# Output projections in two superblocks of tokens, with weight pieces split early and kept in DRAM

## The chip, the cores and the metric

The kernel runs on one core of a Trainium2 chip. The metric is the device time of one execution in microseconds (us). The core has a matrix engine (TensorE, PE in the profile), a vector engine (VectorE, DVE), a scalar engine (ScalarE, ACT), a general engine (GpSimd, POOL), and SyncE (SP), which here only issues transfers. Sixteen DMA engines move data between DRAM and the on-chip memory.

## The reference

One layer of a streaming encoder over 2048 prompt tokens and 32 sample tokens, width 1024, all in fp32. Cut to what matters (`attend` is windowed attention with 8 query and 2 key heads):

```python
(q, k, v, gate_a, b_gate, c_gate, u_in, gate_c, merge_a, merge_c) = jnp.split(h @ w_in, split_idx, axis=-1)
attn, new_k, new_v = attend(q, k, v, sink)                    # q, k normalised and rotated before
conv = ...                                                    # causal, three taps, over c_gate * u_in
y_a = (attn * jax.nn.silu(gate_a)) @ w_attn_out               # 512 -> 1024
y_c = (b_gate * conv * jax.nn.silu(gate_c)) @ w_conv_out      # 512 -> 1024
r = x + (jax.nn.sigmoid(merge_a) * y_a + jax.nn.sigmoid(merge_c) * y_c) @ w_o
r = r + jax.nn.sigmoid(r @ w_ple_gate) * (p @ w_ple_proj)
```

## The kernel before, in words

**Precision and pieces.** Each fp32 product is made of three matmuls on parts of reduced mantissa (fp32r): high weights by high rows, high by low, low by high. So every operand is split: ACT casts the high part, DVE subtracts it to get the low part (the helper at L206 and L207 in phase 1; the planner's operations all stand at one line, L135). A weight piece is 128 x 512 fp32, 256 KB, and serves 12 matmuls per block of tokens. It is loaded raw into one of 8 buffers (`wr`, pool count "wf"), then split into one of 5 tiles (`w`, `WB = 5`).

**Phase 1** (0 to about 855 us) is the big input projection, in two halves of the tokens. It uses a Strassen product (7 block products for 8). The first half runs 21 groups, each of 7 products of 12 matmuls with 512 columns; the second half nests a second level with 264 columns. The order is written by hand (`steps`). At chosen steps (`sums_at`) `quad_sums(x, n)` prepares the Strassen weights of `w_o` (x = UO = 50) and `w_ple_gate` (x = UPG = 58): it loads four quarters, adds them on DVE in four combinations, and stores the four sums to DRAM (`qs`, by POOL's DMA queue). Before, this happens at groups 1 to 8 of the first half.

**Phase 2** (about 855 us to the end) is everything behind. A planner, which runs while the program is built, writes the order of all engines. It keeps a list of events with due times (`begin`), walks the list `plan` of matmul units, and places vector work, transfers and weight loads around them by planned durations and by counts of free buffers. A transfer has a fixed planned time. The units are: yB (the convolution branch), pp (`p @ w_ple_proj`), yA (the attention branch), o (`@ w_o`) and pg (`@ w_ple_gate`). Attention runs as side work, in 17 tiles of 128 tokens (one of them the 32 sample tokens), whose matmuls S (scores), PT (transposes) and O (values) are scattered between the units. A tile's result `at` is stored to DRAM (`z_at`). When a block of tokens is complete, its four rows are loaded again (`acf`), split into `ac_h` and `ac_l` and used by yA of this block.

**Blocks before.** Tokens are cut in four blocks: 512, 512, 512 and 544 (with the sample). Block 0 makes o and pg directly (8 output rows, 8 x 3 matmuls of 512 columns each). Blocks 1 and 2 make a 2 x 2 Strassen product together (`run_big`, `big_done`, `big_end`; matmuls `b50_n_p` for o, `b58_n_p` for pg, product p, output row n; 512 columns). Block 3 makes a Strassen product of its own with 272 columns (`quad_unit`, `run_quads`, `row_quads`; matmuls `s50a` to `s50d` and `s58a` to `s58d`), with the weights loaded and split once more. Both read the sums `qs` from DRAM and split them in phase 2.

Of the kernel before, what the change touches and what calls it, by code (L numbers as in the profile page):

```python
# [13 lines left out]
P = 128  # L14
# [8 lines left out]
BLOCKS = [(0, 512, 0), (512, 512, 0), (1024, 512, 0), (1536, 512, TS)]  # L23
T3 = 1536
W = 512 + TS
# [16 lines left out]
def tile_hybrid_stream_step(ctx: ExitStack, tc: tile.TileContext, x, xT, pT, wu, consts, rope, ckT, cv_dup,  # L42
# [6 lines left out]
    tp = ctx.enter_context(tc.tile_pool(name="tp", bufs=14))  # L49
# [39 lines left out]
    limit = {"ps": 8, "P": 2, "ph": 1, "qs": 1, "q": 1, "r": 1, "z": 1, "ga": 2, "tmp": 14, "wf": 8, "k": KP, "kx": 20, "v": NV // 2 - 1}  # L89
# [98 lines left out]
    def restart():  # L188
        assert not events
        now[0], banks[0], wire[0] = 0.0, 0, None  # L190
        for x in (busy, live):
            for k in x:
                x[k] = 0
        live["k"] = 16
# [75 lines left out]
    BIG = (1, 2)  # L270
    BO = {UO: (2, 7, 1, 6, 5, 3, 4), UPG: (1, 7, 6, 5, 3, 2, 4)}
    NA = {0: range(8), 1: (4, 5, 6, 7, 0, 1, 2, 3), 2: (4, 5, 6, 7, 0, 1, 2, 3), 3: (0, 4, 1, 5, 2, 6, 3, 7)}
    plan = [("yB", e, n) for n in range(8) for e in range(2)]
    for n in range(8):
        plan += [("yB", 2, n), ("yB", 3, n), ("pp", 2, n)]
    plan += [("pp", 3, 0), ("pp", 3, 1)] + [("yA", 0, n) for n in range(5)]
    plan += [("pp", 3, 2), ("yA", 0, 5), ("pp", 3, 3), ("yA", 0, 6), ("yA", 0, 7), ("pp", 3, 4), ("pp", 3, 5)]
# [10 lines left out]
    last_parts = [[(0, 1), (0, 2), (1, 1), (1, 2)]]  # L290
    last_parts += [[x] for x in ((0, 7), (0, 6), (1, 7), (0, 5), (2, 1), (0, 3), (0, 4), (1, 6), (2, 2), (1, 5), (2, 7),
                                 (1, 3), (1, 4), (2, 6), (3, 1), (2, 5), (3, 7), (2, 3), (3, 6), (2, 4), (3, 5), (3, 2),
                                 (3, 4), (3, 3))]

    last_pg = [[(0, 1), (0, 2), (1, 1), (1, 2)]]
    last_pg += [[x] for x in ((2, 1), (2, 2), (0, 7), (0, 6), (1, 7), (0, 5), (1, 6), (0, 3), (1, 5), (0, 4), (1, 3), (2, 7), (1, 4), (2, 6), (3, 1), (2, 5),
                                (3, 7), (2, 3), (3, 6), (2, 4), (3, 2), (3, 5), (3, 4), (3, 3))]
# [24 lines left out]
    worder += [("S", UPG, n, p) for parts in last_pg for n, p in parts]
# [2087 lines left out]
```

## Time and profile before

| what | value |
|---|---|
| median of 3 runs | 1522.86 us (1521.79 to 1523.18) |
| profiled execution | 1523.18 us, of which the span from first to last instruction is 1521.4 us |
| mean granted PE clock | 0.993 of full |
| DMA | 357 MB, mean 235 GB/s |

The busy shares and the stretches are shown in the prediction. In the page, PE is the matrix engine's matmuls and PEld its weight loads, which run beside them; SPq and POOLq are the DMA issues of SyncE and GpSimd. Matmuls are pipelined: the length that the profile shows of one (0.39 us at 512 columns) is longer than the distance to the next one's start, so the distance between starts is what a matmul costs.

### The profile page before, as it was taken

Reading aid. Unit: us, or ns where it says so; the run is one execution under the profiler, and the core shown is the slowest. Engines: PE = TensorE matmul, PEld = TensorE weight load, DVE = VectorE, ACT = ScalarE, POOL = GpSimd, SP = SyncE. Lnnn points to the kernel's source line nnn. Section 1 sums busy time; section 2 is a strip of 40 time slices with the busy share of each in tenths; the row PEclk is TensorE's granted clock in tenths of the full one; section 3 lists DMA queues with packets and bytes.
Section 4 is the critical chain, followed back from the end, with each engine's and each line's share of the span. In section 5 each row is a group of like instructions: output and inputs, shape, how many; then the busy total and the mean of one; then the engine's idle time right before and its main releaser. Section 6 shows DMA issues by size and latency. Waiting matters only on the chain. (4 is left out here: it accounts for less than half of the span.)

```text
span 1521.4 us, 27059 instructions
## 1 busy us (share of the span) xinstructions
PE 1501.7 (99%) x9025; PEld 1334.0 (88%) x9025; DVE 1205.0 (79%) x2291; ACT 835.1 (55%) x1964; POOL 370.3 (24%) x533
## 2 busy tenths in 40 slices
PE   9999999999999999999999999999999999999898
PEld 7878888888889999999999989978888888889898
DVE  7897887875579776898965788789887699786786
ACT  8353254334367634443455557677776476554474
POOL 2133332332212222333223211122122312212112
PEclk9999999999999999999999999989999999999999
DMA  9479886898787946343455797777577947969999
GB/s 343 152 273 342 310 300 221 286 337 273 245 278 260 322 153 197 110 129 123 153 193 188 254 328 221 221 214 229 193 205 213 240 131 175 275 171 298 272 309 258
DMA packets 207004, 357.39 MB, mean 235 GB/s; under 512 B 24592, under 2 KB 61520, under 8 KB 206864
## 3 DMA queue, kind: packets, MB, share of 16 engines
q1 hardware_dynamic: 164928, 251.84, 51.0%
q0 software_dynamic: 32288, 85.99, 19.6%
q10 hardware_dynamic: 9648, 17.83, 3.1%
q8 instruction: 71, 1.16, 0.3%
q14 instruction: 69, 0.57, 0.1%
HBM read 238.21 MB, written 117.46 MB: 234 GB/s over the span
## 5 line engine op out<-in xcount | busy, mean ns | idle before, releaser
L599 PE MATMUL a<-x_l,w 128*128 128x264 f32 (+1 forms) x744 | 228.2, 319 | 0.0
L597 PE MATMUL a<-x_h,w 128*128 128x264 f32 (+1 forms) x744 | 227.2, 320 | 0.0
L602 PE MATMUL a<-x_h,w 128*128 128x264 f32 (+1 forms) x744 | 201.4, 320 | 0.4 <-DVE w L207 0.4
L206 ACT CAST w<-wr 128x512 fp32r<-128x512 f32 (+1 forms) x180 | 110.1, 619 | 104.7 <-PE c L602 28.8
L135 ACT CAST w<-wr 128x512 fp32r<-128x512 f32 x204 | 124.6, 620 | 75.5 <-PE yA L135 17.7
L207 DVE TENSOR_TENSOR w<-wr,w 128x512 fp32r<-128x512 f32 (+1 forms) x180 | 133.8, 753 | 35.2 <-ACT w L206 33.3
L135 DVE TENSOR_TENSOR w<-wr,w 128x512 fp32r<-128x512 f32 x204 | 139.7, 693 | 21.4 <-ACT w L135 18.5
L599 PEld LDWEIGHTS a<-x_l,w 128*128 128x128 f32 x744 | 140.0, 188 | 10.3
L597 PEld LDWEIGHTS a<-x_h,w 128*128 128x128 f32 x744 | 139.7, 188 | 10.4
L135 PE MATMUL b<-xb_h,w 128*128 128x512 f32 x448 | 142.0, 394 | 0.0
L602 PEld LDWEIGHTS a<-x_h,w 128*128 128x128 f32 x744 | 125.2, 188 | 11.2 <-DVE w L207 0.6
L735 PE MATMUL la<-x_h,w 128*128 128x264 f32 x516 | 111.8, 285 | 1.6 <-ACT w L206 1.0
L597 PE MATMUL c<-x_h,w 128*128 128x512 f32 (+1 forms) x336 | 110.5, 339 | 0.1
L599 PE MATMUL c<-x_l,w 128*128 128x512 f32 (+1 forms) x336 | 110.4, 338 | 0.0
L206 ACT CAST w<-a 128x512 fp32r<-128x512 f32 x82 | 49.7, 620 | 95.5 <-DVE a L346 33.2
L602 PE MATMUL c<-x_h,w 128*128 128x512 f32 (+1 forms) x336 | 99.9, 338 | 0.0
L135 PEld LDWEIGHTS b<-xb_h,w 128*128 128x128 f32 x448 | 83.6, 188 | 17.9
L796 DVE SCALAR_TENSOR_TENSOR u<-u,c 128x264 f32<-128x264 f32 (+1 forms) x125 | 59.4, 506 | 43.8 <-ACT u L791 27.3
L135 PE MATMUL yA<-ac_h,w 128*128 128x512 f32 (+1 forms) x320 | 90.4, 360 | 2.3 <-ACT ac_h L135 1.8
L791 ACT COPY u<-a 128x264 f32<-128x264 f32 (+1 forms) x114 | 47.4, 437 | 80.8 <-PE a L602 72.5
L735 PEld LDWEIGHTS la<-x_h,w 128*128 128x128 f32 x516 | 87.0, 189 | 2.2 <-ACT w L206 1.2
L135 PE MATMUL b<-xb_l,w 128*128 128x512 f32 x224 | 88.5, 395 | 0.0
(536 smaller groups left out, 4226.9 us busy)
## 6 DMA issues: line engine op xcount, KB each, us to landing
wr<-in_wu SPq DMA_DIRECT2D x213, 256.0 KB, 4.1
a<-in_wu SPq DMA_DIRECT2D x116, 256.0 KB, 5.1
wr<-ws SPq DMA_DIRECT2D x74, 256.0 KB, 3.4
wr<-qs SPq DMA_DIRECT2D x64, 256.0 KB, 4.8
ws<-a POOLq DMA_DIRECT2D x63, 256.0 KB, 4.0
qs<-a POOLq DMA_DIRECT2D x24, 256.0 KB, 5.8
tb<-z_t SPq DMA_DIRECT2D x24, 256.0 KB, 4.4
z_t<-tb SPq DMA_DIRECT2D x24, 256.0 KB, 4.0
```

The costliest lines, as they stand in the source:

```text
L135: return f(**kw)
L206: nc.scalar.copy(out=hi, in_=src)
L207: nc.vector.tensor_tensor(out=lo, in0=src, in1=hi.bitcast(F32), op=sub)
L597: nc.tensor.matmul(out=ps[:, :cn], lhsT=w[:, 0, k], rhs=x[0][:, c0:c0 + cn], start=first and k == 0, stop=False, skip_group_check=True)
L599: nc.tensor.matmul(out=ps[:, :cn], lhsT=w[:, 0, k], rhs=x[1][:, c0:c0 + cn], start=False, stop=False, skip_group_check=True)
L602: nc.tensor.matmul(out=ps[:, :cn], lhsT=w[:, 1, k], rhs=x[0][:, c0:c0 + cn], start=False, stop=k == 3, skip_group_check=True)
L735: nc.tensor.matmul(out=ps[:, :m], lhsT=w[:, a, k], rhs=r[:, cols], start=q in "ABG" and j == 0 and e == 0, stop=j == 1 and e == 2, skip_gr ...
L791: nc.scalar.copy(out=t[:, c0:c0 + cn], in_=ps[:, :cn])
L796: nc.vector.scalar_tensor_tensor(out=t[:, c0:c0 + cn], in0=t[:, c0:c0 + cn], scalar=-1.0, in1=ps[:, :cn], op0=mul, op1=sub)
```

## The change

1. The blocks become 512, 512, 528 and 528 tokens (`BLOCKS`), the sample inside block 2's and 3's range (`TILES`). The direct o and pg of block 0 and the code of block 3 go. o and pg are Strassen products in two superblocks `s`: blocks 0 and 1 with 512 columns, blocks 2 and 3 with 528 columns in two banks of 264. The order of the seven products changes, with 5 and 3 in pairs, and 1 and 6 too in pg; so do the sums of the results.
2. yB of all four blocks uses one set of 8 weight pieces (before one set for each two blocks). yA now has one set for each block (before blocks 1 and 2 shared one).
3. 44 weight pieces, the 32 quad sums, 8 pieces of `w_attn_out` and 4 of `w_ple_proj`, are split in phase 1 and stored to DRAM as 512 KB with both parts. `quad_sums` moves to every second group from 3 to 17; the new `keep` stands at groups 4 to 15. In phase 2 such a piece is loaded straight into a `w` tile, with no raw buffer and no split.
4. The attention tiles' start times are set anew, the rows `ac` of blocks 2 and 3 are held until a named product begins, the shared temporary pool has 15 buffers for 14, and in the second superblock some residual rows are loaded and added on DVE, where before POOL's accumulating DMA added all of them.

```diff
-BLOCKS = [(0, 512, 0), (512, 512, 0), (1024, 512, 0), (1536, 512, TS)]
+BLOCKS = [(0, 512), (512, 512), (1024, 528), (1552, 528)]
-W = 512 + TS
+W = 532
-    tp = ctx.enter_context(tc.tile_pool(name="tp", bufs=14))
+    tp = ctx.enter_context(tc.tile_pool(name="tp", bufs=15))
...
-    plan += [(kind, 0, n) for kind in ("o", "pg") for n in range(8)]
-    plan += [("yA", b, n) for n in NA[1] for b in BIG]
-    plan += [("B", UO, n, p) for p in BO[UO] for n in range(4)]
...
+    BO = {UO: (2, 1, 6, 7, 5, 3, 4), UPG: (1, 6, 7, 5, 3, 2, 4)}
+    plan = [("yB", b, n) for n in range(2) for b in range(3)] + [("yB", 3, n) for n in range(2)]
+    plan += [("yB", b, n) for n in range(2, 8) for b in range(4)]
+    first, second = products_of(0, UO), products_of(1, UO)
+    def mixed(b, parts):
+        ys = [("yA", b, n) for n in NA[b]]
+        return ys[:6] + [parts[0], ys[6], parts[1], ys[7]] + parts[2:]
+    pps = [("pp", 3, n) for n in range(8)]
+    plan += [("pp", 2, n) for n in range(8)] + pps[:4] + [("yA", 0, n) for n in NA[0]]
+    plan += first[:4] + pps[4:] + mixed(1, first[4:8]) + first[8:] + products_of(0, UPG)
+    plan += [("yA", 2, n) for n in NA[2]] + second[:4] + mixed(3, second[4:8]) + second[8:] + products_of(1, UPG)
...
         for p, o in ((7, "sc"), (5, "a21"), (6, "a11"), (3, "a12")):
-            nc.gpsimd.dma_start(out=quad_sum[x, n][:, WS[p]], in_=t[o])
+            h, lo = high(f"qh{p}_{x}_{n}"), t[o].bitcast(F32R)
+            split(h, lo, t[o])
+            nc.gpsimd.dma_start(out=quad_sum[x, n][:, WS[p], 0], in_=h.bitcast(F32))
+            nc.gpsimd.dma_start(out=quad_sum[x, n][:, WS[p], 1], in_=t[o])
+    def keep(u, e):
+        t, h = tmp(f"kr{u}_{e}")[:, :512], high(f"kh{u}_{e}")
+        nc.sync.dma_start(out=t.rearrange("p (a b) -> p a b", a=4), in_=wu[u, :, 4 * e:4 * e + 4, :])
+        split(h, t.bitcast(F32R), t)
+        nc.gpsimd.dma_start(out=kept[u, e][:, 0], in_=h.bitcast(F32))
+        nc.gpsimd.dma_start(out=kept[u, e][:, 1], in_=t)
...
-    sums_at = {(0, 1 + 2 * n + e, 6): (x, n) for n in range(4) for e, x in enumerate((UO, UPG))}
+    sums_at = {(0, 3 + 2 * (n + 4 * e), 6): (x, n) for n in range(4) for e, x in enumerate((UO, UPG))}
+    keep_at = {(0, 4 + g, 6 if g % 2 else 5): v for g, v in enumerate(kept)}
...
+                w = wp.tile([P, 2, 4, P], F32R, tag="w", name=f"w{i}")
+                W2[i] = w[:, 0], w[:, 1]
+                fin[0] = 0.0
+                eY.dma_start(out=w.bitcast(F32).rearrange("p a b c -> p a (b c)"), in_=stored_at(key))
...
+    def ac_rows(b, j):
+        while b not in ac_open:
+            yield {}
+        yield {"tmp": 1}
+        yield from split_rows(0.5, lambda: ac_pair(b, j), z_at[:, j], ("ac", b, j), b)
+    ac_open = {0, 1}
...
-            t = 11 * g if g < 4 else 33 + (e1 - 98) * (g - 3) / 8 if b < 3 else e1 - 40 + (e2 - 60 - e1) * i / (tiles - 1)
+        t = 11 * e if e < 8 else e1 - 30 + (e2 - e1) * (e - 8) / 9
+    begin.append((T[f"b0{UPG}_0_2"], lambda: ac_open.add(2)))
+    begin.append((T[f"b1{UO}_0_2"], lambda: ac_open.add(3)))
```

What the order of the instructions says at three places. The first is PE before, from the last value matmul of block 0 (O_7) to the first matmul of its yA (`yA0_0`; pp2 and pp3 are pp units of blocks 2 and 3, yB3 one of block 3; pk and pqt are transposes of another attention tile):

```order
L135 MATMUL O_7_11795<-pth_7_0_11679,VH_10072 128x256
...
L135 MATMUL S_10_0_11856<-KH_10068,qs1_1_11746 128x192
...
L135 MATMUL pp2_7_0_11866<-p0_0_h_10677,w375_11306 128x512
...
L135 MATMUL pp3_0_0_11900<-p1_0_h_11501,w377_11604 128x272
...
L135 MATMUL O_8_11959<-pth_8_0_11827,VH_10072 128x256
...
L135 MATMUL pqt1_2_12017<-cst_69,qr1_2_11837 128x128 x4
L135 MATMUL yA0_0_0_11951<-ac0_0_h_12030,w378_11624 128x512
```

After the change other units stand there, and block 1 is the first whose yA comes soon after its last value matmuls (O_15). The same engine, from O_15 to `yA1_0` (b050_3_2 is product 2 of the first superblock's o, row 3):

```order
L136 MATMUL O_15_13081<-pth_15_0_13030,VH_10320 128x256
...
L136 MATMUL b050_3_2_0_13048<-xb050_2_3_h_12851,w382_12899 128x512
...
L136 MATMUL pp3_4_0_13116<-p3_0_h_11997,w383_12938 128x264
...
L136 MATMUL pp3_7_1_13228<-p3_0_h_11997,w384_12960 128x264
...
L136 MATMUL S_18_1_13317<-KH_10316,qs2_1_13268 128x192
...
L136 MATMUL O_16_13332<-pth_16_0_13282,VH_10320 128x256
...
L136 MATMUL yA1_0_0_13241<-ac1_0_h_13293,w385_13004 128x512
```

Between them stand 3 matmuls of 512 columns, 48 pp matmuls of 264 and 37 short ones. The third place is again PE after the change, from the last value matmul of block 3 (O_31) to `yA3_0`:

```order
L136 MATMUL O_31_16305<-pth_31_0_16241,VH_10320 128x256
...
L136 MATMUL yA2_3_1_16294<-ac2_1_h_15627,w452_16069 128x264
...
L136 MATMUL b150_0_2_0_16325<-xb150_2_0_h_16094,w453_16134 128x264
...
L136 MATMUL b150_3_2_1_16442<-xb150_2_0_h_16094,w456_16285 128x264
...
L136 MATMUL yA3_0_0_16479<-ac3_0_h_16475,w457_16333 128x264
```

Between them stand the last 7 matmuls of a yA2 unit and the 96 of product 2. In phase 1, POOL's DMA queue, first before, where the four sums of one quad are stored among the stores of phase 1's own sums (`ws`):

```order
L350 DMA ws2_118<-sc2_1088 128x512
L615 DMA z_q_77<-u40_0_1076 128x512
L350 DMA ws2_118<-a2_1_1082 128x512
L364 DMA qs50_0_137<-sc_50_0_1122 128x512
L350 DMA ws2_118<-a2_0_1080 128x512
L364 DMA qs50_0_137<-a21_50_0_1116 128x512
```

The same queue after, at a later group:

```order
L360 DMA qs50_0_137<-qh7_50_0_1384 128x512
L361 DMA qs50_0_137<-sc_50_0_1379 128x512
L360 DMA qs50_0_137<-qh5_50_0_1389 128x512
L360 DMA qs50_0_137<-qh6_50_0_1394 128x512
L361 DMA qs50_0_137<-a21_50_0_1373 128x512
L628 DMA z_q_77<-u20_2_1265 128x512
```

Each sum now makes two stores, the high and the low part, and the store of the low part stands behind the DVE subtraction.

More of the change, by code (lines that the diff above doesn't have):

```diff
@@ L1365, in attention @@
         fin[0] = max(fin[0], ab_done)
-        yield {"tmp": 1} if last and i >= 3 else {}
+        yield {"tmp": 1} if out else {}
         for q, (h0, hn, src) in enumerate(q3):
@@ L1382, in attention @@
             eS.copy(out=h, in_=src)
-        if last and i >= 3:
+        if out:
             vo = tmp(f"vo{i}", cols=P)
@@ L1412, in attention @@
         yield {"ps": 2, "qs": 1}
-        if last and i >= 3:
+        if out:
             ko = kso[P - TS:P] if sample else kpo
@@ L2057, in tile_hybrid_stream_step @@
[L2057 to L2076 removed]
+            loads = [("pp", z_pp[n + 4 * i])]
@@ new lines, in big_unit @@
+            if s and (n == 3 and p in (2, 4) or p == 4):
+                loads.append(("rs", z_r[n + 4 * i]))
+        units.append(dict(b=2 * s + j, n=n, p=p, x=x, s=s, kind="B", name=f"b{s}{x}_{n}_{p}", w=[("B", s, x, n, p)],
+                          act=[()] * 4, loads=loads, got=0))
+    def run_big(u):
+        s, x, n, p = u["s"], u["x"], u["n"], u["p"]
+        g = big[s, x, n]
+        subs = blk(2 * s)[2]
+        floor[0] = 3 * len(subs)
+        fresh = p != 3 and (p != 6 or x == UO)
+        if not fresh:
+            while ("e", s, x, n, {6: 1, 3: 5}[p]) not in have:
+                idle()
+        if fresh:
+            pss = []
+            for e, (c0, cn) in enumerate(subs):
@@ L2079, in run_quads @@
                 banks[0] += 1
-                g[new] = bank(f"s{x}{new}_{n}")
-        for k in range(4):
-            for (n, p), wk in zip(u["parts"], u["w"]):
-                wi = w_of(wk, u)
-                i, half = XP[p]
-                while ("X", x, i, k) not in have or w_ready.get(wi, 1e9) > now[0]:
+                pss.append((bank(f"b{s}{x}_{n}_{p}_{e}"), c0, cn))
+            if p in (1, 5):
+                g["a"] = pss
+        else:
+            pss = g["a"]
+        wk, = u["w"]
@@ L2086, in run_quads @@
+        wi = w_of(wk, u)
+        for y, (ps, c0, cn) in enumerate(pss):
+            for k in range(4):
+                while ("XB", s, x, p, k) not in have or w_ready.get(wi, 1e9) > now[0]:
                     idle()
-                ps = groups_of[x, n]["d" if (n, p) == (3, 4) else {2: "b", 7: "c", 4: "c"}.get(p, "a")]
-                fresh = p in (1, 2, 7) or (n, p) == (3, 4)
                 hi, lo = [v[:, k] for v in W2[wi]]
-                xs = [v[:, half * m:(half + 1) * m] for v in XQ[x, k][i]]
@@ L2091, in run_quads @@
[L2091 to L2100 removed]
+                xh, xl = XB[s, x, p, k]
@@ new lines, in run_big @@
+                for e, (w, r) in enumerate(((hi, xh), (hi, xl), (lo, xh))):
+                    while begin and begin[0][0] <= work[0]:
+                        begin.pop(0)[1]()
+                    eT.matmul(out=ps[:, :cn], lhsT=w, rhs=r[:, c0:c0 + cn], start=fresh and k == 0 and e == 0,
+                              stop=k == 3 and e == 2, skip_group_check=True)
+                    work[0] += 0.00044 * cn + 0.0064
+                    due()
+                if n == 3 and y == len(pss) - 1:
+                    free("k", 2)
+                    free("kx", 2)
```

714 lines of the change are left out of this document (201 added, 513 removed).

## The prediction

> **What bounds the kernel now.** The page comes first: TensorE (PE) is busy 99% of the span. Then the windows view, because an average over the span hides where the rest is lost. PE's issue sets the time almost everywhere.
>
> ```profile
> span 1521.4 us, 27059 instructions
> PE 1501.7 (99%) x9025; PEld 1334.0 (88%) x9025; DVE 1205.0 (79%) x2291; ACT 835.1 (55%) x1964; POOL 370.3 (24%) x533
> ```
>
> ```profile
> core 0: us, PE busy (x) PEld busy (x) DVE busy (x) ACT busy (x) POOL busy (x), PEclk, DMA share, GB/s
> 60.00:100.00 40.00, 39.90 (x170) 31.46 (x169) 39.23 (x65) 23.61 (x44) 7.72 (x15) 1.00 0.50 175
> 100.00:140.00 40.00, 40.00 (x175) 32.54 (x174) 29.38 (x47) 14.43 (x26) 15.01 (x29) 1.00 0.95 342
> 220.00:260.00 40.00, 40.00 (x176) 32.31 (x175) 30.93 (x52) 19.17 (x44) 9.95 (x18) 1.00 0.64 219
> 260.00:300.00 40.00, 40.00 (x174) 32.46 (x174) 34.33 (x55) 12.39 (x22) 12.80 (x25) 1.00 0.79 277
> 300.00:340.00 40.00, 40.00 (x174) 32.39 (x174) 32.72 (x53) 17.13 (x30) 13.89 (x26) 1.00 0.95 333
> 340.00:380.00 40.00, 40.00 (x175) 32.40 (x174) 22.99 (x39) 18.02 (x32) 9.14 (x17) 1.00 0.83 281
> 996.00:1010.00 14.00, 10.91 (x39) 7.15 (x37) 8.56 (x19) 9.52 (x29) 0.00 (x0) 0.63 0.46 148
> 1368.00:1420.00 52.00, 52.00 (x317) 46.89 (x316) 36.31 (x71) 21.51 (x39) 13.24 (x16) 1.00 1.08 304
> 1420.00:1436.00 16.00, 11.40 (x68) 10.42 (x66) 15.06 (x30) 8.91 (x17) 2.62 (x3) 0.79 0.79 219
> ```
>
> Each row is a stretch: its length, busy us and instructions of each engine, granted clock, DMA share and rate. Two stretches lose time. At 996 us PE idles 14.00 - 10.91 = 3.1 us and has clock 0.63, which costs up to 14 x 0.37 = 5.2 us more. At 1420 us it idles 4.6 us and has clock 0.79, another 16 x 0.21 = 3.4 us. Together 16.3 us. The waits view of PE names them (us in total, times, longest):
>
> ```profile
> PE s50a L135 <- DVE w L135: 2.5, 1, 2.5
> PE yA L135 <- ACT ac_h L135: 1.8, 2, 1.3
> PE s50b L135 <- DVE w L135: 1.4, 1, 1.4
> PE s58b L135 <- DVE w L135: 0.5, 1, 0.5
> ```
>
> The first stretch is yA of block 0, which waits for the block's attention rows; the second is the start of block 3's o products, whose weights are not split yet.
>
> **Part 1: PE's issue.** Timeline rows of a dense 512-, 264- and 272-column stretch (start, length, instruction), then groups by form:
>
> ```profile
> 119.96 0.39 PE L597 MATMUL c<-x_h,w 128*128 128x512 f32 x1
> 120.19 0.39 PE L599 MATMUL c<-x_l,w 128*128 128x512 f32 x1
> ...
> 499.76 0.28 PE L735 MATMUL la<-x_h,w 128*128 128x264 f32 x1
> 499.88 0.29 PE L735 MATMUL la<-x_l,w 128*128 128x264 f32 x1
> ...
> 1449.91 0.29 PE L135 MATMUL s50a<-rq_h,w 128*128 128x272 f32 x1
> 1450.04 0.29 PE L135 MATMUL s50a<-rq_l,w 128*128 128x272 f32 x1
> ...
> L135 PE MATMUL b<-xb_h,w 128*128 128x512 f32 x448 | 142.0, 394 | 0.0
> L135 PE MATMUL s50a<-rq_h,w 128*128 128x272 f32 x128 | 28.3, 298 | 2.6 <-DVE w L135 2.5
> L135 PE MATMUL o<-m_h,w 128*128 128x512 f32 x128 | 42.3, 399 | 0.0
> ```
>
> Starts lie 0.23 us apart at 512 columns, 0.12 at 264, 0.13 at 272; the mean over all dense pairs of the trace is 0.2313, 0.1218 and 0.1253. The direct o and pg of block 0 are 2 x 192 = 384 matmuls of 512 columns (128 with o's high rows, 64 with the low ones, pg alike), block 3's Strassen products 672 of 272 columns. That is 88.7 + 84.0 = 172.7 us. Now blocks 2 and 3 make 1344 matmuls of 264 columns, 164.0 us, while the 672 of 512 columns (b, high and low) stay. Gain 8.7 us. Blocks 2 and 3 are now both 528 tokens in two banks, so yA and yB pay two 264s for some 512s, +0.7 us each, pp +0.3 us. **PE: -7.0 us.**
>
> A rule speaks against this term. The Trainium skill, "TensorE: Matmul & The Clock Gate", section "Back-to-back issue gap", gives about 131 ns per matmul sustained at 512 columns and 81 at 128; an estimate on the line between them is 99 ns at 264 and 272, by which the exchange would cost some 15 us (384 x 131 + 672 x 99 = 117, then 1344 x 99 = 133) instead of gaining 9. This trace does not agree: its 512s start 231 ns apart.
>
> **Part 2: the two old stalls.** In the changed order yA of block 0 comes after pp of blocks 2 and 3; PE has 20.5 us of matmuls between the block's last attention output and yA (before 10.3 us). The S start is gone; its quarter of the weights arrives split. Both stretches: **-16.3 us.** Other waits for split weights of that stage: **-1.3 us.**
>
> **Part 3: the new places of the same wait.** The chain from the last O matmul to the first yA matmul, block 0, then block 1:
>
> ```profile
> 986.22 0.28 PE L135 MATMUL O<-ptl,VH 128*128 128x256 f32 x1
> 986.99 0.56 SPq L135 DMA_DIRECT2D z_at<-at  x1
> 993.62 0.38 SPq L135 DMA_DIRECT2D acf<-z_at  x1
> 999.39 0.79 PE L135 MATMUL yA<-ac_h,w 128*128 128x512 f32 x1 [1.35 <-ACT ac_h L135]
> 1005.25 0.80 PE L135 MATMUL yA<-ac_l,w 128*128 128x512 f32 x1 [0.33 <-DVE ac_l L135]
> ...
> 1077.12 0.28 PE L135 MATMUL O<-ptl,VH 128*128 128x256 f32 x1
> 1089.97 0.65 ACT L135 ACTIVATE ac_h<-acf 128x512 fp32r<-128x512 f32 x1
> 1094.49 0.63 ACT L135 ACTIVATE ac_h<-acf 128x512 fp32r<-128x512 f32 x1
> ```
>
> It goes through DRAM (store, load, split) and takes 13.2 us to the first matmul in block 0; in block 1 13.5 us (1090.62, when ac_h is done), and 18.7 us to the last low row (1094.49 + 0.63 + about 0.7). In the changed order PE has after block 1's last O only 36 + 12 pp matmuls of 0.122, 3 of 0.231 and 37 short ones of about 0.11 before yA: 11.6 us. The fourth row is needed 3 x 0.69 us and one PT later, at 14.4 us: it is 4.3 us late. Block 3 has 7 yA and 96 b matmuls: 103 x 0.122 = 12.6 us; its fourth row is needed at 13.7 us, 5.0 us late. Block 0's 8.3 us had a gap of 10.3 us; there the fourth row (19.7 us after O) was needed at about 13.4 with the O in between, 6.3 us late, so the slowed clock added about 2 us net. With that, 6.3 and 7.0 us: **+13.3 us.** Ends: 0, if the chain runs 5 us shorter; +17, if both cost what block 0 cost.
>
> The Trainium skill, same page, section "HAM oscillation — how this bites in real kernels", has the clock fall only after PE idles more than about 3.4 us; waits of 1 to 2 us with matmuls between would leave it at full, and the two stalls would cost 9.3 us. The row at 996 us does not agree: clock 0.63 with no single wait over 1.35 us. It is kept as a rival below.
>
> **Part 4: the early splits.** Phase 1 gets 44 ACT casts and 44 DVE subtractions, 56 more POOL DMAs and 12 more SP loads, off PE's path while buffers last. The rows that price them:
>
> ```profile
> L207 DVE TENSOR_TENSOR w<-wr,w 128x512 fp32r<-128x512 f32 (+1 forms) x180 | 133.8, 753 | 35.2 <-ACT w L206 33.3
> wr<-in_wu SPq DMA_DIRECT2D x213, 256.0 KB, 4.1
> wr<-qs SPq DMA_DIRECT2D x64, 256.0 KB, 4.8
> qs<-a POOLq DMA_DIRECT2D x24, 256.0 KB, 5.8
> ```
>
> The sums move from groups 1 to 8 (about 83 to 225 us) to every second group from 3 to 17 (122 to 400 us; a group is 7 x 12 x 0.231 = 19.4 us). Per pair of groups DVE gets 4 adds, 4 + 2 subtractions, 10 x 0.6 = 6 us; so 260:300 goes from 34.3 to 40 of 40 us and its neighbours to 37 and 39. At 60:100 DVE had 39.2 of 40 and PE lost 0.1 us. The DMA gets per pair 18 x 0.262 = 4.7 MB in 38.8 us, 122 GB/s: 277 becomes 399, 333 becomes 455, 281 becomes 403. Scaled by their rows' shares these are 1.14, 1.30 and 1.19, against 1.08 at 1368:1420 with no PE loss. The excess is (3.63 - 3.24) x 40 = 16 us of DMA time. Eight raw buffers, each a piece of 12 x 0.231 = 2.8 us, less 4 us of landing, hide up to 18 us if only loads lag; the pieces summed in phase 1 and the splits have less. Ends 0 and +14; nearer 0, as buffers and the DVE row say: **+5 us.**
>
> **Part 5: pre-split loads in phase 2.** The stored pieces go by one 512 KB load straight into one of 5 tiles, without the 8 raw ones ahead. Lead: 4 x 2.77 - 0.6 = about 10.4 us. 256 KB land in 4.1 to 4.8 us by the medians above; 512 KB in about 6 by doubling the bytes' part. Late only in the crowded stretches. The ACT and DVE work they save is not on the path. SP waits for a tile's release with whatever stands behind, the attention's rows among it. Ends 0 and +10: **+2 us.** yB with one set of weights saves 8 loads and splits; hidden, 0.
>
> **Part 6: the tail.**
>
> ```profile
> 1516.08 0.29 PE L135 MATMUL s58a<-rq_h,w 128*128 128x272 f32 x1
> 1517.38 0.44 DVE L135 TENSOR_TENSOR tg<-tg,rs 128x272 f32<-128x272 f32 x1
> ```
>
> The last output row is now 528 wide after the last product instead of 272: tanh and two DVE steps at 0.65 to 0.70 (ac_h's 512 took 0.65) for 0.43 to 0.44, plus a combine: **+0.9 us.**
>
> **Sum:** -7.0 - 16.3 - 1.3 + 13.3 + 5 + 2 + 0.9 = -3.4. The profiled execution took 1523.2 us, 0.3 above the median, so 1519.8, or about **1519.5** on the median's footing.
>
> **Rivals.**
> (a) The new waits stay away. The store and reload take 5.4 us in block 1 but 6.6 in block 0; ACT and DVE are freer, and SP has fewer loads in the queue. If the rows come 5 us sooner, 13.3 us go: 1506. Against it: two blocks gave 13.2 and 13.5 us at different loads.
> (b) Slower: the DMA excess at 260 to 380 us reaches the weights. It decides from the point where pieces land more than 18 us after issue, or DVE's queue is over 6 us behind. Then phase 1 pays the 14 of its upper end: 1519.5 + 9 = 1528.5. For it: 455 GB/s against 342, the highest of the rows. Against: most of the excess is stores, which nothing awaits.
> (c) Pre-split pieces come late, +10 instead of +2: 1527.5. Against: the share 1.08 stretch, though with raw buffers.
> (d) By the clock rule the new stalls cost no slow clock: 4 us less, 1515.5.
>
> **How the numbers follow.** A measurement here tells 0.2%, 3 us, from no change; faster is below 1519.8, slower above 1525.9. The forecast, 1519.5 (own range 1514 to 1525), has 0.40; it is faster in half of that, else same. (a) 0.15, faster. (b) 0.22: slower 0.15, same 0.04, faster 0.03. (c) 0.13: slower 0.06, same 0.04, faster 0.03. (d) 0.10: faster 0.09, same 0.01. Faster 0.20 + 0.15 + 0.03 + 0.03 + 0.09 = 0.50; same 0.20 + 0.04 + 0.04 + 0.01 = 0.29; slower 0.21. The range 1505 to 1531 leaves out a third of (a) below and a quarter of (b) and (c) above.
>
> **What would show it.** Right: PE's starts 0.122 us apart in the second superblock; no idle window at yA of block 0 nor at the second o's start; a wait of yA on ac_h with a clock near 0.6 to 0.8 at yA of blocks 1 and 3; DMA share above 1.05 at 260 to 380 us with PE nearly 40 of 40. Wrong: PE waiting in phase 1 on DVE's or ACT's w (b), in phase 2 on a DMA into w (c), or yA of blocks 1 and 3 without a wait (a).

## The result, and the profile after

The changed kernel takes 1559.13 us (median of 4 runs, 1557.03 to 1566.39) against 1522.32 us: the ratio is 1.0255, interval 1.0217 to 1.0292. The forecast was 1519.5, range 1505 to 1531. The profiled execution is the fastest of the four, 1557.03 us with a span of 1555.3 us, 33.9 us longer than before. Where they lie, by common points of the two traces (of the last matmul, its start):

| stretch | before | after | difference | forecast of the same |
|---|---|---|---|---|
| to the first yB matmul (phase 1) | 855.5 | 882.1 | +26.7 | +5 |
| first yB to last matmul (phase 2) | 660.6 | 666.0 | +5.4 | -9.3 |
| last matmul to end | 5.3 | 7.1 | +1.8 | +0.9 |

The page of after, and its windows, beside the stretches shown of before. 225 to 345 us is where phase 1 loses most; the last rows are the stalls of phase 2:

```profile
span 1555.3 us, 27890 instructions
PE 1508.1 (97%) x9553; PEld 1357.2 (87%) x9553; DVE 1188.7 (76%) x2274; ACT 788.6 (51%) x1877; POOL 403.0 (26%) x590
```

```profile
280.00:320.00 40.00, 33.11 (x132) 25.30 (x132) 29.92 (x48) 9.36 (x18) 12.82 (x25) 0.96 0.90 313
320.00:360.00 40.00, 35.02 (x136) 27.13 (x135) 31.70 (x51) 16.69 (x30) 16.08 (x30) 0.91 1.00 364
1005.00:1042.00 37.00, 33.16 (x248) 31.07 (x247) 27.83 (x62) 31.95 (x110) 4.61 (x3) 0.95 0.89 292
1095.00:1108.00 13.00, 9.37 (x49) 7.37 (x47) 8.78 (x18) 10.16 (x35) 1.55 (x3) 0.87 0.93 341
1325.00:1340.00 15.00, 9.88 (x63) 9.26 (x62) 4.25 (x11) 4.25 (x16) 1.70 (x2) 0.81 1.08 324
```

Before, PE had 40.00 of 40 in every window of phase 1 from 100 to 380 us. Now it has 33.11 and 35.02, with fewer matmuls (132 and 136, before about 175). By the windows no other engine is full there: DVE has 29.92 and 31.70 of 40 us, where before it had 35.80 and 26.68. The DMA moves 313 GB/s at share 0.90, then 364 at 1.00; a share of 1.08 cost PE nothing at 1368 to 1420 us of before. But these are averages beside a PE that is slowed down, and they don't say that no engine is at its limit. Two longer rows, before and after, divided by PE's matmuls, say more:

```profile
225.00:345.00 120.00, 120.00 (x522) 97.18 (x521) 95.54 (x152) 49.93 (x98) 35.27 (x66) 1.00 0.81 280
225.00:345.00 120.00, 106.79 (x431) 82.77 (x430) 99.60 (x161) 50.08 (x99) 49.22 (x92) 0.96 0.92 333
```

Before, DVE works 95.54 / 522 = 0.183 us for each matmul. After, it is 99.60 / 431 = 0.231, as much as the distance of two matmuls: at PE's full pace DVE would have no time left. The waits say who waits for whom. PE's waits in 225 to 345 us of after, then one of them in the timeline (start, length, instruction, idle time before it and its releaser), PE's rows first, then DVE's and ACT's:

```profile
PE a L610 <- ACT u L804: 8.1, 3, 4.0
PE a L610 <- ACT w L207: 2.2, 1, 2.2
PE a L610 <- ACT s L804: 2.1, 3, 0.9
```

```profile
308.01 0.40 PE L615 MATMUL c<-x_h,w 128*128 128x512 f32 x1
312.42 0.50 PE L610 MATMUL a<-x_h,w 128*128 128x512 f32 x1 [4.01 <-ACT u L804]
...
301.68 0.77 DVE L516 SCALAR_TENSOR_TENSOR b<-b,cst,rb 128x528 f32<-128x528 f32 x1 [0.39 <-DMA b<-in_xT]
...
306.33 0.68 DVE L335 TENSOR_TENSOR sc<-a,a 128x512 f32<-128x512 f32 x1
...
308.14 0.70 DVE L520 TENSOR_TENSOR T<-b,b 128x528 f32<-128x528 f32 x1
308.76 0.68 DVE L336 TENSOR_TENSOR a<-a,a 128x512 f32<-128x512 f32 x1
309.36 0.70 DVE L521 TENSOR_TENSOR b<-b,b 128x528 f32<-128x528 f32 x1
309.98 0.68 DVE L337 TENSOR_TENSOR a<-a,a 128x512 f32<-128x512 f32 x1
310.75 1.14 ACT L207 CAST w<-a 128x512 fp32r<-128x512 f32 x2 [7.27 <-DVE a L337]
311.79 0.58 ACT L804 COPY u<-a 128x512 f32<-128x512 f32 x1
```

Read from the end: PE wants a bank that ACT's copy `u<-a` (L804) has to empty. The copy stands in ACT's queue behind the cast of a weight sum, which waits 7.27 us for DVE's add (L337). That add is itself late on DVE. The three quarters that it needs had landed by 300.40 us. But DVE runs its instructions in the order of its queue and has no gap from 301.7 to 313 us, and steps of the preparation of the second half's rows stand ahead of the first add (`b<-b,cst,rb`, L516) and between the adds (`T<-b,b` and `b<-b,b`, L520 and L521). So three queues that run in order pass one lateness on, and at this wait, the longest in the window, it comes from DVE's queue and not from a late input. Inputs do land later on the whole. At PE's 2.07 us of waiting that end at 287.2 the third quarter landed 8.5 us after its issue, at 283.9, and DVE's second add began right behind it. Landing of all `a` quarters issued between 225 and 345 us, before and then after (there with the quarters of the early sums):

```profile
DMA to landing us min/median/max: 2.3/4.2/8.4
```

```profile
DMA to landing us min/median/max: 2.5/5.7/10.6
```

The experiments below show that this median alone does not decide.

### The profile page after: what moved, and what is told of

Same layout as the page of the kernel before. It is cut to its first block, busy times and chain, and to the rows that moved or that the text cites. A ratio compares the mean times of both kernels' runs of the same rounds, so it can differ in the third digit from the quotient of the medians.

```text
span 1555.3 us, 27890 instructions
## 1 busy us (share of the span) xinstructions
PE 1508.1 (97%) x9553; PEld 1357.2 (87%) x9553; DVE 1188.7 (76%) x2274; ACT 788.6 (51%) x1877; POOL 403.0 (26%) x590
## 4 chain that ended last, share of the span: by engine, by line
PE 61%; DMA 8%; DVE 4%; issue 3%; ACT 3%; SPq 1%; POOL 0%; ACTq 0%; DVEq 0%; POOLq 0%
PE b L136 17%; PE yB L136 6%; PE a L610 5%; PE a L615 5%; PE la L748 5%; PE a L612 5%; PE yA L136 4%; PE lc L748 2%; PE c L610 2%; PE c L615 2%; PE c L612 2%; PE O L136 1%; DMA wr<-in_wu 1%; DMA acf<-z_at 1%; PE lb L748 1%
## 5 line engine op out<-in xcount | busy, mean ns | idle before, releaser
L136 PE MATMUL b<-xb_h,w 128*128 128x264 f32 (+1 forms) x1344 | 310.6, 322 | 1.7 <-DVE c L136 1.0
L610 PE MATMUL a<-x_h,w 128*128 128x264 f32 (+1 forms) x744 | 230.4, 323 | 13.6 <-ACT u L804 8.1
L136 PEld LDWEIGHTS b<-xb_h,w 128*128 128x128 f32 x1344 | 222.7, 188 | 20.4 <-DVE c L136 1.6
L136 PE MATMUL b<-xb_l,w 128*128 128x264 f32 (+1 forms) x672 | 216.5, 322 | 0.4 <-DVE xb_l L136 0.3
L615 PE MATMUL a<-x_h,w 128*128 128x264 f32 (+1 forms) x744 | 203.1, 323 | 0.0
L207 ACT CAST w<-wr 128x512 fp32r<-128x512 f32 (+1 forms) x180 | 110.2, 618 | 100.4 <-PE la L748 30.1
L136 PEld LDWEIGHTS b<-xb_l,w 128*128 128x128 f32 x672 | 126.4, 188 | 10.0 <-DVE xb_l L136 1.0
L136 PE MATMUL yA<-ac_h,w 128*128 128x264 f32 (+1 forms) x384 | 93.9, 330 | 4.3 <-DMA w<-kw 2.1
L136 PE MATMUL yB<-ycs_h,w 128*128 128x264 f32 (+1 forms) x384 | 90.6, 324 | 0.0
L804 ACT COPY u<-a 128x264 f32<-128x264 f32 (+1 forms) x114 | 47.2, 436 | 69.5 <-PE a L615 68.8
```

The source lines that it names most:

```text
L136: return f(**kw)
L207: nc.scalar.copy(out=hi, in_=src)
L610: nc.tensor.matmul(out=ps[:, :cn], lhsT=w[:, 0, k], rhs=x[0][:, c0:c0 + cn], start=first and k == 0, stop=False, skip_group_check=True)
L615: nc.tensor.matmul(out=ps[:, :cn], lhsT=w[:, 1, k], rhs=x[0][:, c0:c0 + cn], start=False, stop=k == 3, skip_group_check=True)
L804: nc.scalar.copy(out=t[:, c0:c0 + cn], in_=ps[:, :cn])
```

## The experiments

Lateness is counted against the profile of before: at the start of the 1200th of phase 1's 4992 projection matmuls (342 us in before), at the 1600th (435 us), and at the first yB; phase 2 is from there to the last matmul. What is lost at a place of phase 2 is the time between matmul starts beyond their dense distances. The lateness of each run comes from one trace. Kernels that share their phase 1 differ by 2.5 us at the first yB (after and lead_only) and by 4.2 us (spread_fill, spread_pp and spread_fill_raw23), and the four executions of the changed kernel lie 9.4 us apart, so a few us between single runs mean nothing.

| run | at 1200 | at 1600 | first yB | phase 2 | time | ratio (interval) |
|---|---|---|---|---|---|---|
| after | 22.6 | 25.6 | 26.7 | 666.0 | 1559.13 | 1.0255 (1.0217 to 1.0292) |
| raw_late | 5.4 | 5.7 | 7.0 | 693.3 | 1565.01 | 1.0289 (1.0260 to 1.0318) |
| raw_work | 17.5 | 17.8 | 18.9 | 692.3 | 1575.22 | one run |
| dup | 27.0 | 33.1 | 36.2 | 664.7 | 1564.87 | one run |
| dup_small | 15.2 | 18.0 | 16.9 | 667.6 | 1549.5 | one run |
| old_places | 27.4 | 27.7 | 27.3 | 663.2 | 1556.12 | 1.0228 (1.0206 to 1.0250) |
| act_queue | 37.6 | 52.2 | 52.7 | 666.7 | 1583.3 | one run |
| second_half | 1.7 | 2.1 | 20.2 | 665.2 | 1550.52 | 1.0197 (1.0180 to 1.0214) |
| second_half_nokeep | 1.6 | 1.9 | 23.8 | 668.3 | 1555.61 | 1.0227 (1.0207 to 1.0248) |
| sums_only | 18.8 | 25.3 | 25.8 | 668.9 | 1558.31 | one run |
| rows_later | -0.4 | 48.6 | 50.6 | 666.4 | 1581.31 | one run |
| spread_fill | 1.7 | 6.9 | 12.2 | 660.9 | 1544.58 | 1.0152 (1.0043 to 1.0262) |
| spread_pp | 0.0 | 5.0 | 11.5 | 662.5 | 1539.22 | 1.0117 (1.0088 to 1.0146) |
| spread_fill_raw23 | 3.4 | 8.5 | 15.7 | 660.5 | 1538.81 | 1.0114 (1.0078 to 1.0150) |
| lead_only | 23.7 | 28.0 | 29.2 | 661.9 | 1555.04 | one run |
| spread2_fill_lead | 2.1 | 2.4 | 15.8 | 662.3 | 1542.01 | 1.0138 (1.0117 to 1.0160) |
| spread2_pp_lead | 1.5 | 1.8 | 14.9 | 658.5 | 1537.51 | 1.0115 (1.0090 to 1.0139) |
| pitch544 | 29.9 | 37.4 | 38.7 | 663.0 | 1566.0 | one run |
| tmp16 | 23.4 | 33.6 | 36.9 | 665.4 | 1566.43 | one run |

**Is it the split work, the bytes, or the place?**

```diff
 raw_late: raw sums, nothing kept (and phase 2 loads and splits all pieces)
-            h, lo = high(f"qh{p}_{x}_{n}"), t[o].bitcast(F32R)
-            split(h, lo, t[o])
-            nc.gpsimd.dma_start(out=quad_sum[x, n][:, WS[p], 0], in_=h.bitcast(F32))
-            nc.gpsimd.dma_start(out=quad_sum[x, n][:, WS[p], 1], in_=t[o])
+            nc.gpsimd.dma_start(out=quad_sum[x, n][:, WS[p], 0], in_=t[o])
...
```

> The changed kernel with no early split: the four sums of a quad are stored raw (half the bytes) at the new places, groups 3 to 17, no other piece is kept, and phase 2 loads all pieces raw and splits them. In the changed kernel the first 1600 matmuls of phase 1 end 26 us later than before. Theory W (the 44 casts and subtractions hold up ACT's and DVE's queues) and theory B (the 18 MB more of transfers do) both expect phase 1 within 3 us of before; theory P (the place alone: adds and stores at groups 9 to 17 meet the preparation of the second half's rows) expects it 10 us or more late. Phase 2 says what the superblocks alone do: if they do what I forecast, the whole time is 1510 to 1530.

Phase 1 is 7.0 us late, 4.9 of it between 320 and 360 us: more than W or B expected, less than P. The whole was expected at 1510 to 1530 if the superblocks do what I forecast, and took 1565.01. The surprise is phase 2: without stored splits it takes 693.3 us, 27 us more than in the changed kernel. So the superblocks with raw pieces would have been slower still; I had put that saving at 0. In phase 2 DVE is 61 us busier and ACT 55 than in the changed kernel.

```diff
 raw_work: raw_late, and in phase 1 (the kept pieces alike)
+            h = high(f"qh{p}_{x}_{n}")
+            nc.scalar.copy(out=h, in_=t[o])
+            nc.vector.tensor_tensor(out=h, in0=t[o], in1=h.bitcast(F32), op=sub)
...
```

> As raw_late, but phase 1 also does the 44 casts and 44 subtractions (and the 12 loads) of the changed kernel, into a tile that nobody reads or stores: the work without the bytes. Phase 2 splits once more. Theory W: phase 1 is late by 15 to 26 us, as in the changed kernel. Theory B: late by at most 5 us.

18.9 us: 12 more than raw_late, for the splits and the 12 loads. Theory W gets its number.

```diff
 dup: no splits, each piece stored twice (the kept pieces alike)
-            h, lo = high(f"qh{p}_{x}_{n}"), t[o].bitcast(F32R)
-            split(h, lo, t[o])
-            nc.gpsimd.dma_start(out=quad_sum[x, n][:, WS[p], 0], in_=h.bitcast(F32))
+            nc.gpsimd.dma_start(out=quad_sum[x, n][:, WS[p], 0], in_=t[o])
             nc.gpsimd.dma_start(out=quad_sum[x, n][:, WS[p], 1], in_=t[o])
...
```

> The changed kernel without the casts and subtractions of phase 1: every sum and kept piece is stored twice as it is, so the bytes and the number of stores are those of the changed kernel, and the low parts that phase 2 reads are not low parts. Theory W: phase 1 within 5 us of before. Theory B: late by 15 to 26 us. Phase 2 has the same order as the changed kernel, within 3 us.

36.2 us, so theory B gets its number too. That it is more than the changed kernel's 26.7 is not shown: its 1564.87 us lie among the changed kernel's own times, 1557.03 to 1566.39. The two do not add: each alone makes phase 1 late. In 225 to 345 us DVE has 0.200 us of work for each matmul here, so a DVE without any time left is not needed for the loss.

```diff
 dup_small: dup, second store of each pair only
+            nc.gpsimd.dma_start(out=quad_sum[x, n][:, WS[p], 1, :64], in_=t[o][:, :64])
...
```

> As dup (no split work in phase 1, each piece stored twice by POOL's queue), but the second store of each pair moves only 64 of 512 columns; phase 2 reads the first store into both parts, so that the low parts are not low parts. The number and the order of the stores on POOL's queue are those of dup. Phase 1 of dup is 36 us late. Theory B (bytes): it falls to 10 to 20 us, raw_late having 7. Theory Q (the stores stand in POOL's queue ahead of phase 1's own stores and wait for loads there): it stays at 30 us or more.

16.9 us: taking away 7/8 of 44 stores' bytes, 10 MB, gives 19 us back. The number and order of stores alone are not the cause (theory Q would be 30), but 10 us stay over raw_late.

```diff
 act_queue: this store and the three others, 88 in all
-            nc.gpsimd.dma_start(out=quad_sum[x, n][:, WS[p], 0], in_=h.bitcast(F32))
+            nc.scalar.dma_start(out=quad_sum[x, n][:, WS[p], 0], in_=h.bitcast(F32))
...
```

> The changed kernel with the 88 stores of split pieces issued on ACT's queue instead of POOL's; bytes, work and places are the same. Theory Q: phase 1 loses 10 us less than the 26 of the changed kernel, or better. Theory B: it stays within 6 us of 26; a little more is possible, since ACT issues 88 more transfers.

52.7 us late. A store of a low part waits on ACT for DVE, and PE's evictions wait behind it: ahead of 203.57 and 247.25 us ACT stands idle for 7.2 and 7.3 us behind such stores, and PE then waits 3.7 and 4.7 us for ACT. A queue with evictions in it is the wrong place. The run refutes Q's remedy, and shows the chain of queues again.

```diff
 old_places
+    sums_at = {(0, 1 + 2 * n + e, 6): (x, n) for n in range(4) for e, x in enumerate((UO, UPG))}
...
 second_half
+    sums_at = {(1, 2 + 2 * (n + 4 * e), 6): (x, n) for n in range(4) for e, x in enumerate((UO, UPG))}
+    keep_at = {(1, 3 + g, 5): v for g, v in enumerate(kept)}
```

> The changed kernel with the quad sums, their splits and stores back at groups 1 to 8, one each, so that 8 adds and splits of DVE and 3.1 MB fall on every group there; the 12 kept pieces stay at groups 4 to 15. Theory P: phase 1 loses less than 10 us, since groups 9 to 17 carry only kept pieces. Theories W and B: the loss moves to 85 to 230 us and is at least as large, 20 us or more.

The loss moves and stays as large: 17.4 us at matmul 600 (202 us), where the changed kernel has 0.7. P as stated fails: one quad a group is too much, one every two groups at 3 to 7 is not.

> The changed kernel with all of the early work (quad sums, splits, kept pieces, their 88 stores) moved to the second half of phase 1, at groups 2 to 16 (sums) and 3 to 14 (kept pieces) there, where the trace of before moves 110 to 220 GB/s instead of 220 to 340. If the loss of phase 1 is a matter of the place, where loads are needed just in time and the DMA is crowded (theory B), it falls from 26 us to under 5 and the whole to about 1535. If the work on DVE or ACT is what costs (theory W), the second half, where DVE is 60 to 90% busy, loses 15 us or more too.

The first half is now 2.1 us late, so the early work is what costs there. But the second half loses 18 us between 600 and 800 us, where PE waits for DVE's sums of its nested products and DVE has 38 to 39 of 40 us between 640 and 760: theory W expected 15 us or more there. In total it is 8.6 us better than the changed kernel, not the 24 of theory B.

> As second_half, but only the 32 quad sums are split early; the 8 pieces of yA and the 4 of pp are loaded raw into the 8 raw buffers and split in phase 2, as before the change. Theory L (the 512 KB loads without a raw buffer come late at yA of block 2, 9 us of loss around 1330 us): that stall goes, and phase 2 is 5 to 9 us shorter than in second_half. If the splits on ACT and DVE are what phase 2 can't bear there: 5 us or more longer.

Phase 2 is 3.1 us longer; neither 5 to 9 shorter nor 5 or more longer came. The stall around 1330 us shrinks from 9.4 to 3.0 us but 1080 to 1160 us loses 8.7 more.

**What in groups 9 to 14?**

> The changed kernel with only the 32 quad sums split early, at its own places; the 8 pieces of yA and 4 of pp are not kept (12 loads, 12 splits and 24 stores fewer in phase 1) and are loaded raw in phase 2. If the kept pieces' loads and stores, which stand on SP's and POOL's queues between phase 1's own, carry the loss: phase 1 late by 7 to 12 us, as with raw sums. If the sums' doubled stores and splits carry it: 20 us or more. If bytes count in proportion (a third fewer): about 17.

25.8 us, in one run: the kept pieces carry little of it or none (at matmul 1200 it is 18.8 where the changed kernel is 22.6).

```diff
 spread_fill
+    places = [(0, 1, 6), (0, 3, 6), (0, 5, 6), (0, 7, 6), (0, 15, 6), (0, 17, 6), (0, 19, 6), (1, 3, 6)]
...
+    places = [(0, g, 5) for g in (2, 4, 6, 8, 16, 18, 20)] + [(1, g, 5) for g in (2, 4, 5, 6, 7)]
...
-        return ys[:6] + [parts[0], ys[6], parts[1], ys[7]] + parts[2:]
+        return [parts[0]] + ys[:7] + [parts[1], ys[7]] + parts[2:]
```

> The changed kernel with the early work spread: sums at groups 1, 3, 5, 7, 15, 17, 19 of the first half and 3 of the second, kept pieces at 2, 4, 6, 8, 16, 18, 20 and five early groups of the second half. Groups 9 to 14, where all variants lost most, carry none. And one unit of product 1 of o (12 matmuls) goes ahead of yA of blocks 1 and 3 as filler. Theory N (not the amount, but meeting the preparation of the second half's rows at groups 9 to 14, decides): phase 1 late by under 8 us. Theory A (amount): 15 us or more. Filler: the stalls at yA of blocks 1 and 3 shrink by 2 to 3 us each, phase 2 about 661.

The first `places` are the sums, the second the kept pieces. At matmul 1400 it is 2.2 us late where the changed kernel is 25.9. It has done less by then, though: 58 of the 88 stores are issued, where the changed kernel has issued all. With the rest, 4.7 us are lost at groups 17 to 20 and 5.3 more after. The 12.2 us at the end lie between theory N (under 8) and theory A (15 or more): the place explains more than half of the loss, not all. The stalls at yA of blocks 1 and 3 shrink from 6.7 to 2.2 and from 2.8 to 0 us, but 3.1 us come back at 1120 to 1160 and 4.2 at 1200 to 1240; phase 2 is 660.9. The two timed runs lie far apart (1537.58 and 1551.59), hence the wide interval.

```diff
 rows_later
-    prep = [at_step[0, g, 7] for g in range(7, G)]
+    prep = [at_step[0, g, p] for g in range(14, G) for p in (7, 5)]
```

> The changed kernel with the preparation of the second half's rows (4 loads, some 12 DVE steps and 7 stores a step) moved from one step a group at groups 7 to 20 to two a group at groups 14 to 20; the early work stays at groups 3 to 17. If the meeting of the two is the cause, phase 1 is late by under 4 us until group 13 (matmul 1200, where the changed kernel is 22.6 us late) and loses after that, at groups 14 to 20. If groups 9 to 14 are too full by themselves, it is 15 us or more late at matmul 1200 as before.

This is the cleanest of them. The window 225 to 345 us of rows_later, beside the two rows shown above; at matmul 1200 it has issued 69 of the 88 early stores, the changed kernel 68:

```profile
225.00:345.00 120.00, 119.92 (x518) 96.62 (x517) 87.18 (x142) 55.86 (x109) 35.64 (x68) 1.00 0.80 279
```

PE has 119.92 of 120 us and the lateness at matmul 1200 is -0.4, against 22.6. So neither the early work nor those groups are too much; meeting the row preparation is. After group 14, where the row preparation is now twice as dense and the last early work stands, it loses 49 us; 11.4 of them are one wait for the rows themselves, which come too late for the second half. The run takes work out of the window, so it shows that the two do not fit there together, not which engine or queue is short.

What goes with the loss in this window is how long ACT's cast of a weight sum waits for DVE's third add. The longest of these waits is 4.2 us in before, 4.8 in raw_late, 3.0 in rows_later and 3.4 in spread_fill, where PE has 115.8 to 120.0 of 120 us. It is 7.3 us in after, 7.0 in raw_work, 7.6 in dup and 8.1 in dup_small, where PE has 106.0 to 110.2. The median landing time does not tell them apart: it is 5.0 us in rows_later, which loses nothing, and 5.0 in raw_work, which is 17.5 us late. At the longest of these waits the third add ends 10.3 us after its inputs have landed in after, 11.7 in raw_work and 10.3 in dup_small, most of it spent in DVE's queue; before, the most was 6.3. But rows_later has 9.5 once without a loss, so this alone does not decide either.

> The changed kernel with 16 buffers in the temporary pool instead of 15, paid for by one row buffer less (40 instead of 41); the planner's limits follow only for the rows, so phase 2 may differ by a few us. If phase 1 loses because sums and row preparation run out of temporary buffers: it is 12 us or less late at matmul 1600 where the changed kernel is 25.6 (pitch544, with 14, is the other point of the line). If the pool's size isn't it, and pitch544 lost its 12 us otherwise: 22 us or more.

> The changed kernel with the operand rows in tiles of 544 columns, as before the change, instead of 528, and the temporary pool back at 14 buffers to make room (which changes the planner's order in phase 2). If the place of the moving rows in memory sets it, the 512-column matmuls of phase 1 start 231.3 ns apart again (232.4 in the changed kernel, 2.0 us over phase 1); if not, they stay at 232.3 to 232.5.

These two asked whether the meeting happens in the shared temporary pool. With 14 buffers phase 1 is 38.7 us late, with 16 it is 36.9, with 15 it was 26.7: neither count gives the time back, so the pool's size is probably not it. Each is one run, and each changes the row buffers too. Their times, 1566.0 and 1566.43, lie at the slow end of the changed kernel's own (up to 1566.39), so that they are worse is not shown. Whether DVE's queue, the DMA's landing times or SP's queue carries the meeting over the whole window stays open.

**Phase 2.**

> As spread_fill, with pp of block 2 between the units of yB and pp of block 3 between those of yA of block 0, as before the change, instead of twelve pp units in a row. If the row of short pp units with attention beside it overloads ACT and DVE (PE's waits around 1010 to 1040 us, 6.9 us), that stall goes and phase 2 is about 5 us shorter than in spread_fill; if not, within 2 us or longer.

The losses at 1000 to 1040 us shrink from 5.1 to 1.2 us as expected, but 1080 to 1120 grows from 2.2 to 7.1 and 1280 to 1320 from 0 to 7: 662.5, no gain.

> As spread_fill, but yA of blocks 2 and 3 loads its weights raw, into the 8 raw buffers, and splits them; blocks 0 and 1 keep the split pieces. Theory L (late 512 KB loads at yA of block 2): the 9 us stall there shrinks to 3 or less and phase 2 is 4 to 6 us shorter than in spread_fill. Otherwise within 2 us, or longer for the 16 more splits.

Theory L fails: with raw weights the stall at yA of block 2 is 6.3 us against 7.3 in spread_fill. A reason is in DVE's timeline of after, at that place:

```profile
1322.90 0.42 DVE L136 TENSOR_TENSOR ptl<-PT,pth 128x256 fp32r<-128x256 f32 x1
1328.27 0.43 DVE L136 SCALAR_TENSOR_TENSOR tk<-tk,yA 128x264 f32<-128x264 f32 x1 [4.95 <-DMA tk<-z_t]
...
1334.65 0.43 DVE L136 SCALAR_TENSOR_TENSOR tk<-tk,yA 128x264 f32<-128x264 f32 x1 [4.35 <-DMA tk<-z_t]
1335.00 1.01 DVE L136 TENSOR_TENSOR ptl<-PT,pth 128x512 fp32r<-128x512 f32 x2
```

```profile
1332.58 0.36 PE L136 MATMUL yA<-ac_h,w 128*128 128x264 f32 x1 [2.10 <-DMA w<-kw]
1335.74 0.58 PE L136 MATMUL O<-ptl,VH 128*128 128x256 f32 x1 [2.19 <-DVE ptl L136]
```

DVE waits twice for the row `tk` that yA's result is multiplied with, 9.3 us in all, and the attention's low part `ptl`, for which PE waits, stands behind. Landing of `tk` from 1290 to 1345 us:

```profile
DMA to landing us min/median/max: 6.8/8.6/15.2
```

```diff
 lead_only
-    LEAD, LOOK = 2, 11
+    LEAD, LOOK = 3, 11
```

> The changed kernel with the rows of a phase 2 unit (tk, pp and others) loaded three units ahead instead of two, nothing else. Theory R (the tk rows land up to 15 us after issue around 1310 to 1340 us, DVE waits for them 9.3 us there with the attention's low parts behind it): the stall of 9.1 us at yA of block 2 shrinks to under 3, and phase 2 is 5 us or more shorter than 666.0. Otherwise (DMA too crowded at any lead, or the earlier loads crowd others): within 2 us of it.

DVE's waits for `tk` in phase 2 fall from 14.1 to 2.7 us, and phase 2 to 661.9. But PE's waits for late weights there grow from 2.1 to 4.7 us:

```profile
DVE tk L136 <- DMA tk<-z_t: 2.7, 1, 2.7
```

```profile
PE yA L136 <- DMA w<-kw: 4.7, 4, 2.4
```

The loss at 1320 to 1360 us, yA of block 2, falls from 9.1 to 5.8 us, not to under 3, and phase 2 by 4.1 us, not by 5 or more. So theory R names one wait, and the crowded DMA (share 1.08 at 1325:1340 in after) probably hands it on to the weights.

> spread_fill with groups 9 to 14 and 17 to 20 free of early work (sums at 1, 3, 5, 7, 15 of the first half and 3, 6, 9 of the second; kept pieces at 2, 4, 6, 8, 16 and at 2, 4, 5, 7, 8, 10, 11), and with the rows loaded three units ahead. Phase 1 should be late by 4 to 7 us instead of 11.5, phase 2 at 650 to 656 if theory R holds: 1520 to 1528 in all, about the time of before. If both fail, 1535 or more.

> As spread2_fill_lead, with the pp units of blocks 2 and 3 between those of yB and yA as in spread_pp, where the waits at 1010 to 1040 us shrank from 5.1 to 1.2 us but 1280 to 1320 lost 7. With the rows earlier: 3 to 5 us shorter than spread2_fill_lead, 1517 to 1523; if the stalls only move, within 2 us of it.

The first half of phase 1 is clean at 2.4 and 1.8 us, and the second half then loses 13 us with the three sums and seven kept pieces there. Phase 2 is 662.3 and 658.5, where 650 to 656 was expected of the first. Rows three units ahead didn't mend yA of block 2 here either: 6.8 and 5.7 us are lost at 1320 to 1360, with PE's waits for late weights at 4.5 and 3.0. The two forecasts, 1520 to 1528 and 1517 to 1523, were missed by 14 us or more; that the second kernel is 3 to 5 us shorter than the first came true (4.5). The fastest version, spread2_pp_lead, is 22 us better than the changed kernel and still 1.0115 (1.0090 to 1.0139) of before. No version here beats before.

**A small thing by the way.** 512-column matmuls start 231.3 ns apart on the mean in before. In the changed kernel it is 232.4 in phase 1 and 233.1 in phase 2, also at 30 to 200 us, where little differs but the place of things in memory. pitch544 (rows of 544 columns again) has 231.4 and 232.1, tmp16 (528, one row buffer less) 231.7 and 232.2. Nine other runs with the changed kernel's layout of tiles have 232.2 to 232.4 in phase 1. So the distance goes with the layout in memory, and not with the rows' pitch alone. 264-column matmuls stay at 121.7 to 121.9.

## Why the prediction was wrong, point by point

- **PE's issue, -7.0.** The count is right: by the distances of before, the issue of all matmuls falls by 8.0 us. The 512s are dearer by 1.1 and 1.8 ns (1849 and 973 dense pairs), +3.8 us, 2.0 of it in phase 1. Net -4.2. The trace's 264-column distance held (121.8 and 121.9 ns).
- **The old stalls, -16.3.** Half right. The S start is gone. At yA of block 0 the rows `ac` are no longer late, but PE loses 6.9 us between 1000 and 1040, just ahead of it and at its start: twelve pp units in a row beside the attention, with ACT busy 31.95 of 37 us, waits for banks that DVE and ACT have to empty (2.3 us on DVE's `tt`), and clock 0.95. I looked only at the wait that I knew and not at what would stand there.
- **The same wait at yA of blocks 1 and 3, +13.3.** 6.7 and 2.8 us were lost there. At block 3 it is the wait I named, but smaller (7.0 forecast):

```profile
1371.93 0.39 PE L136 MATMUL yA<-ac_h,w 128*128 128x264 f32 x1 [1.38 <-ACT ac_h L136]
```

  At block 1 PE stops just before yA, on another one:

```profile
1100.86 0.36 PE L136 MATMUL S<-KH,qs 128*128 128x192 f32 x1 [2.10 <-DVE qs L136]
```

  That is attention's own chain, on an ACT that is busy 10.16 of 13 us. The size (6.3 forecast) was right by luck, as the wait is another. The working has a slip there, too: PE's 11.6 us of matmuls after block 1's last O do not come out of 37 short ones, which give 10.6; the trace has 45, which give 11.5. The clock did fall there (0.87 in 1095:1108) with no single wait over 2.1 us, so rival (d), by which it would stay full, falls at block 1; at block 3 the clock stayed at 1.00. The Trainium skill, "TensorE: Matmul & The Clock Gate", section "HAM oscillation — how this bites in real kernels", asks for an idle gap of some 3.4 us; the row of 1095:1108 does not agree.
- **The early splits, +5.** The step that failed: 26.7 us, 2.0 of it the dearer 512s. My range for it ended at 14. I had both of its parts, DVE near full and DMA demand above what the trace had shown, and then let the buffers absorb it ("nearer 0, as buffers and the DVE row say"). That row, 60 to 100 us, has as much DVE work for each matmul as 225 to 345 us of after (39.23 / 170 = 0.231 us) and loses 0.1 us, but its DMA moves 175 GB/s and not 333. I added loads of engines over 40 us windows. What counts is that a weight sum is made just in time by a chain DMA, DVE, ACT, PE through queues in order: some steps of DVE ahead of an add, or a load that lands late, stop ACT, and with it PE's evictions. At the longest wait it was DVE's queue; which link decides over the whole window stays open. Rival (b) named the place (260 to 380 us) and the mechanism of the late queue; it would have had phase 1 pay 14 us, half of what came. Its point, DVE's queue over 6 us behind, is met: ACT waited 7.27 us for one add. The other, landing more than 18 us after issue, is not: 10.6 was the longest.
- **Pre-split loads, +2.** yA of block 2 lost 9.1 us. PE's waits for late weights were 2.1 of it; late `tk` rows are the likely cause of much of the rest, but when lead_only took their waits away 5.8 us stayed, on late weights. The 512 KB loads landed in 4.9 and 5.4 us by their medians (`w<-qs` and `w<-kw`), sooner than the 6 I had put, but in 9.3 at 1290 to 1345 us. Rival (c) had the stage (crowded DMA) and one of the two victims. And the saving of splits, which I called hidden, is worth 27 us in phase 2, by raw_late.
- **Phase 2 as a whole.** The time lost there beyond dense distances rose by about 9 us, from 20.9 to 29.7, where my terms for it sum to -2.3 (-16.3 - 1.3 + 13.3 + 2). The old stalls went, and new ones came in other places.
- **The tail, +0.9.** +1.8: behind the last matmul stand two combining adds of 264 columns, where I counted one step, before the 528 row is finished and stored.

## What to carry to other kernels

Before adding work to a stretch that is full on PE, look for the chain that is just in time there (who waits for whom by how little), and price the new work as delay on that chain and not as busy time of its engines. When a stall is moved, ask what the new neighbours need of the same engines: here a filler of short matmuls brought its own evictions. If two pieces of side work use the same queues, keep them apart: rows_later and spread_fill each gave back over 20 us at matmul 1200 by moving one of the two away. The work has to fit where it goes, though: rows_later lost 49 us and spread_fill 10 after that.

## What was unexpected of the hardware

The distance of 512-column matmuls is 231.3 to 233.2 ns between kernels and goes with the layout of their tiles in memory, while 264-column ones do not change. The rise from before to after costs 3.8 us here. That the place of the operands does it is likely but not isolated, and which address property it would be wasn't tried.
